# State-space layer of a two-layer backbone: two groups on the partition halves, real and imaginary parts along the free axis

## The chip, the cores and the metric

The kernel is one program on one core of a Trainium2 chip. The metric is the device time of one execution in microseconds (us), lower is better. The core has a matrix engine (TensorE; PE in the profile, PEld for its weight loads), a vector engine (VectorE, DVE), a scalar engine (ScalarE, ACT), GpSimd (POOL) and a sync engine (SP) that issues most of the DMAs here. Each engine works through its own instructions in program order and waits on semaphores for the others. Data lies in SBUF, 128 partitions wide. Products of the matrix engine land in PSUM, 128 partitions of 4096 fp32 columns, in eight banks of 512 columns.

## What is computed

A latent stream of 1024 tokens and a context of 256 tokens, model width 1024, run through two layers: a differential attention with an MLP, and a bidirectional S5 state-space mixer with a gated output (GLU) and an MLP. The change touches the S5 mixer only. Cut to it, the reference is

```python
S5_GROUP, S5_GROUPS, S5_STATE = 16, 64, 64          # 16 channels x 64 groups, 64 complex states a group
lam_bar = exp(lam * dt);  b_bar = ((lam_bar - 1) / lam)[..., None] * (b_re + 1j * b_im)
def step(h, uc):                                     # over chunks of time, forwards and backwards
    bu = einsum('gpc,btgc->btgp', b_bar, uc)
    hs = scan(a=lam_bar, b=bu) + a_cum * h           # h[t] = lam_bar * h[t-1] + bu[t]
    y = real(einsum('gcp,btgp->btgc', c_mat, hs))
y_lat = glu(y_forward + y_backward + d_skip * h_lat) # gelu, one matrix product, o1 * sigmoid(o2)
```

Context tokens are run ahead of the latent ones in each direction; the output is the latent stream.

## The kernel before

The program first does the attention layer, and beside it, on engines that are free, it makes tables for the S5 mixer and writes them to DRAM: `s5_prep` (decay and angle of each state), `s5_tables` (a record per set of four groups, `recd`: input weights X, output weights W), `s5_phases` (integer phases, `ptd`). The last part of layer 0 is its second MLP product, in whose time most of these tables are made. Then comes `s5()`, then `glu()` and the MLP of layer 1.

`s5()` turns time into eight parts of 128 steps, which are laid along the columns of a tile `U`, and treats the 64 groups in 16 sets of four. One turn `n` of its loop (L1811 and on) does a set; turns overlap, so turn `n` holds pieces of sets `n-2` to `n+1`. The steps are written out by hand inside `self.manual()`, so their order in the code is the order on each engine. Direction `d` is 0 (forwards) or 1 (backwards). In a turn:

- `inputs(n, d)` (PE, L1755): products of the input weights with the columns of U, 160 columns a group, into the two 1024-column areas `xbank` of PSUM. One area gets the real and imaginary part, the other the same with the halves swapped. Both directions use both areas in turn.
- `phase` (POOL, L1738) makes integer phases of 128x640, `trig` (ACT, L1742 to L1744) makes sine and cosine of them, in three steps.
- `rotate(n, d)` (DVE, L1764 and L1766) multiplies the two areas by cosine and sine; POOL adds the two (L1848, L1856).
- `decay(n, d)` (ACT, L1771) writes the decay of each state into the 640 PSUM columns `r` (2048 to 2687), and `scan(n, d)` (DVE, L1775) reads them there and runs the recurrence. I write S0 and S1 for the scans of direction 0 and 1 of a turn.
- `back` (DVE L1787, POOL L1785) turns the states back by the phases.
- `outputs(n-1)` (PE): for each of four groups one product with the lag table (L1793) and four with the states of the set before (L1796), into bank 6 or 7 of PSUM by the parity of the turn.
- gelu of set `n-2` out of that bank: square (ACT L1833), L1843 on DVE, tanh and a copy (ACT L1844, L1850), the product L1864 on DVE.
- `tr` (PE, L1800): four transposes of gelu's result into the same bank, from where `tr_out` copies a high part (ACT L1804) and a low part (DVE L1805) to SBUF, in the next turn.
- In turns 8, 10, 12, 13, 14, 15, 16 and 17, `ada_half_products` (L270 to L281): 32 products of 32 columns for the modulation vectors of layer 1, a copy (ACT L273), a transpose (L274) and up to three small DVE steps.

Beside it, `load_x` and `load_w` bring the next record from DRAM (SP). PE's order at the end of a turn is `outputs(n-1)`, `inputs(n+1, 0)`, the modulation products, `tr`; `inputs(n, 1)` comes early in the next turn.

Waits between engines are set by a scheduling layer from the accesses that the program makes. Which waits it sets is seen in the lists of instructions in the section on the change.

Of the kernel before, what the change touches and what calls it, by code (L numbers as in the profile page):

```python
# [13 lines left out]
KB = 256  # L14
# [56 lines left out]
class Prog:  # L71
# [83 lines left out]
    def setup(self):  # L155
# [15 lines left out]
        self.r8 = c.tile([128, 128], F32, name="r8")  # L171
# [814 lines left out]
    def s5_prep(self):  # L986
# [60 lines left out]
        ts(dup[:, 1, 1], zi, -1.0, None, ALU.mult)  # L1047
        b = self.misc.next()
        pc = fv(5.5, 128)
        for j in range(2):  # L1050
            nc.tensor.transpose(b[:, 128 * j : 128 * j + 128], dup[:, j].rearrange("p a b -> p (a b)"), self.ident)
        v.tensor_copy(self.r8, b[:, 0:128])
        ts(pc, b[:, 128:256], PHASE, None, ALU.mult)
# [96 lines left out]
    def s5_tables(self, o, w, acc, acc2):  # L1150
# [21 lines left out]
        def matrices(i):  # L1172
            (tp, tc_, tb_), W, XT, q = ins[i % 3], Wr[i % 2], XTr[i % 2], todo[i]
            tt(W, bcast(tc_[:, :, 0:16], 2, 9), bcast(tp[:, :, 0:9], 3, 16), ALU.mult)
            tt(t4, bcast(tc_[:, :, 16:32], 2, 9), bcast(tp[:, :, 9:18], 3, 16), ALU.mult)
            tt(W, W, t4, ALU.add)
            d = q // 16
            w0 = 1 - d
            self.dma(shaped(self.recd[q % 16][:, 1536 + 512 * d : 2048 + 512 * d], (4, 128)),
                     W[:, :, w0 : w0 + 8].rearrange("p x i c -> p x (i c)"))  # L1180
# [55 lines left out]
    def s5_phases(self, o):  # L1236

        nc = self.nc
        g = nc.gpsimd.tensor_tensor
        B, P, P16 = (self.fv(x, *d).bitcast(I32) for x, d in ((o, (128, 16)), (o + 8, (128,)), (o + 8.5, (128,))))  # L1240
        self.dma(self.fv(o + 9, 128), self.phd)
        nc.vector.tensor_copy(P, self.fv(o + 9, 128))
# [452 lines left out]
    def s5(self):  # L1695
# [10 lines left out]
        rx = shaped(r, (4, 160))  # L1706
        At, Bt = self.fv(42.5, 128, 10).bitcast(I32), self.fv(47.5, 128, 16).bitcast(I32)
        A0, B0 = self.hv(46, 2, 4, 10).bitcast(I32), self.hv(47, 2, 4, 16).bitcast(I32)
        phs = [(self.fv(x, 4, 160), self.fv(x + 2.5, 4, 160)) for x in (0, 7.5, 24.5)]
        ts = [[(self.fv(x, 4, 160), self.fv((12.5, 20)[d], 4, 160)) for x in ((5, 29.5), (15, 17.5))[d]] for d in range(2)]  # L1710
        cs = [[(self.fv(x, 4, 128), self.fv(y, 4, 128)) for x, y in (((5, 32), (29.5, 34)), ((15, 22.5), (17.5, 22.5)))[d]]
              for d in range(2)]
        slots = []
        for b in (self.hv(64, 4096).bitcast(F32), self.wv(0, 4096)):
            slots.append((shaped(b[:, 0:1536], (2, 4, 192)), shaped(b[:, 1536:2560], (2, 4, 128)),
                          shaped(b[:, 2560:3072], (4, 128)), shaped(b[:, 3072:4096], (2, 4, 128)), b))
        gT = self.gT = self.hgroups()[0:2]
        x_first = self.hv(40, 1536).bitcast(F32)
# [5 lines left out]
        def load_x(n):  # L1724
            self.dma(slots[n % 2][4][:, 0:1536] if n else x_first, self.recd[n, :, 0:1536])

        def load_w(n):
            b = slots[n % 2][4]
            self.dma(b[:, 1536:2560], self.recd[n, :, 1536:2560])
            self.dma(b[:, 2560:3072], self.lagd[:, 512 * n : 512 * n + 512])  # L1730
            for h in range(2):
                self.dma(b[64 * h : 64 * h + 64, 3072:4096], self.recd[n, 64 - 64 * h : 128 - 64 * h, 1536:2560])

        def phase(n, d):

            x0, P = 64 * d + 4 * n, phs[(2 * n + d) % 3][0].bitcast(I32)
            a, b = (At[:, x0 : x0 + 4], Bt[:, x0 : x0 + 4]) if n else (A0[:, d], B0[:, d])
            pool.tensor_tensor(P.rearrange("p x (a b) -> p x a b", b=16), bcast(a, 3, 16), bcast(b, 2, 10), ALU.add)  # L1738

        def trig(n, d):  # L1740
            Ps, Pc = phs[(2 * n + d) % 3]
            act.activation(Pc, Ps.bitcast(I32), AF.Sin, scale=0.5 * UNPHASE)  # L1742
            act.activation(Ps, Ps.bitcast(I32), AF.Sin, scale=-UNPHASE)
            act.activation(Pc, Pc, AF.Square, scale=float(np.sqrt(2.0)))  # L1744

        xbank = [self.PS[:, 1024 * j : 1024 * j + 1024] for j in range(2)]

        def inputs(n, d):
            X = slots[n % 2][0] if n else shaped(x_first, (2, 4, 192))
            cols = slice(0, 160) if d == 0 else slice(32, 192)  # L1750
            for j in range(2):
                b = xbank[j]
                for i in range(4):
                    o = 176 * i
                    mm(b[:, o : o + 160], X[:, d, i, 64 * j : 64 * j + 128], U[:, 4 * n + i, cols], start=True, stop=True)  # L1755

        def rotate(n, d):
            (Ps, Pc), (t1, t2) = phs[(2 * n + d) % 3], ts[d][n % 2]
            for j, (t, P) in enumerate(((t1, Pc), (t2, Ps))):
                b = xbank[j]  # L1760
                x = bass.AP(b.tensor, b.offset + (159 if d else 0),
                            [list(b.ap[0]), [176, 4], [-1 if d else 1, 160]])
                if j:
                    v.tensor_tensor(t, x, P, ALU.mult)  # L1764
                else:
                    v.scalar_tensor_tensor(t, P, -1.0, x, ALU.add, ALU.mult)  # L1766

        def decay(n, d):

            x0 = 64 * d + 4 * n  # L1770
            act.activation(rx[:, :, 1:160], bcast(r8[:, x0 : x0 + 4], 2, 159), AF.Copy)  # L1771

        def scan(n, d):
            t1, t2 = (t.rearrange("p x n -> p (x n)") for t in ts[d][n % 2])
            v.tensor_tensor_scan(t2, r, t1, 0.0, ALU.mult, ALU.add)  # L1775

        def back(eng, n, d, j):
            Ps, Pc = phs[(2 * n + d) % 3]
            o = cs[d][n % 2][j]
            if d:  # L1780
                o = bass.AP(o.tensor, o.offset + 127, [list(o.ap[0]), [128, 4], [-1, 128]])
            h = slice(31, 159)
            t2 = ts[d][n % 2][1][:, :, h]
            if j:
                eng.tensor_tensor(o, t2, Ps[:, :, h], ALU.mult)  # L1785
            else:
                eng.scalar_tensor_tensor(o, Pc[:, :, h], -1.0, t2, ALU.add, ALU.mult)  # L1787

        def outputs(n):
            X, W1, T, W2, _ = slots[n % 2]  # L1790
            for i in range(4):
                o = self.bank(6 + n % 2)[:, 128 * i : 128 * i + 128]
                mm(o, U[:, 4 * n + i, 32:160], T[:, i], start=True, stop=False)  # L1793
# [4 lines left out]
        def tr(kb, g, b):  # L1798
            for i in range(4):
                nc.tensor.transpose(b[:, 128 * i : 128 * i + 128], ggs[kb % 2][:, 4 * g + i].rearrange("p g c -> p (g c)"), self.ident)  # L1800

        def tr_out(kb, g, b):
            hi, lo = gT[g][0][:, kb], gT[g][1][:, kb]
            act.activation(hi, b, AF.Copy, scale=0.5)  # L1804
            return lambda: v.scalar_tensor_tensor(lo, b, 0.5, hi.bitcast(F32), ALU.mult, ALU.subtract)  # L1805

        for t, c0, w in ((A0, 0, 10), (B0, 5 * KB, 16)):
            self.dma(t, self.ptd[:, c0 : c0 + 128 * w].rearrange("p (d x w) -> p d x w", d=2, w=w)[:, :, 0:4])

        load_x(0)  # L1810
        self.dma(self.fv(42.5, 13 * KB).bitcast(I32), self.ptd)  # L1811
        load_w(0)
        self.act_set("silu_and_others")
        with self.manual():
            act.activation(U[:, :, 160:192], U[:, :, 0:32], AF.Copy)
            v.memset(rx[:, :, 0:1], 0.0)
# [4 lines left out]
            inputs(0, 0)  # L1821
            load_x(1)
            load_w(1)
            for n in range(19):
                run, m = n < 16, n - 2
                gelu = 0 <= m < 16
                bank, other = self.bank(6 + n % 2), self.bank(7 - n % 2)
                y = shaped(bank, (4, 8, 16))
                lo = tr_out((n - 4) // 2, n % 2, other) if n >= 4 else None
# [15 lines left out]
                if run:  # L1845
                    inputs(n, 1)
# [27 lines left out]
                if n < 15:  # L1874
                    inputs(n + 1, 0)
                for i, (a, b) in enumerate(mods):
                    if n == b:
                        self.ada_half_products(halves[i % 2 if i > 2 else 0], 1, 2 + i // 2, i % 2, self.PS[:, 1856:1984])
                if n + 1 < 16:
                    phase(n + 1, 1)  # L1880
                if 3 <= n < 19:
                    tr((n - 3) // 2, 1 - n % 2, bank)
# [7 lines left out]
            tr_out(7, 1, bank)()  # L1890
# [402 lines left out]
```

## Time and profile before

| | |
|---|---|
| median of 3 runs | 2930.72 us (2928.89 to 2932.73) |
| the profiled execution | 2930.97 us |
| its span, first to last instruction | 2929.2 us (1.77 us less) |
| mean granted TensorE clock | 0.985 |
| PE busy | 2793.7 us (95%) |
| DVE, ACT, POOL busy | 1899.8, 1309.7, 1012.6 us |
| `s5()`, first input product to the first GLU split | 1906.87 to 2105.84 us |

A row of the timeline gives the start, the duration, engine, line, operation, the tile written and those read with their shapes, how many instructions were joined to the row, and in brackets how long the engine had been idle before it and what ended that. `PS` is PSUM, `FD` and `U` are tiles in SBUF. A row of the windows gives a stretch of time, its length, the busy time of each engine with its count of instructions, the granted clock of the TensorE (PEclk), and the share and rate of the DMA engines.

### The profile page before, as it was taken

What the parts mean: (1) busy time and instruction counts of PE and PEld (TensorE: products, weight loads), DVE (VectorE), ACT (ScalarE), POOL (GpSimd) and SP (SyncE); (2) the same over time, 40 slices, a digit from 0 to 9 for tenths busy, and PEclk for the clock granted to TensorE, in tenths of its full rate; (3) what the DMA queues carried; (4) which work ended last, traced back from release to release, by engine and by line L of the source; (5) the groups of instructions that cost most, each with busy time, mean ns of one, the idle gap of its engine ahead of it and who ended that gap; (6) DMA issues with size and microseconds to landing.
All of it is one profiled execution on the core that took longest, in us unless ns stands there. A gap on an engine that the chain in (4) does not pass through costs nothing.

```text
span 2929.2 us, 44409 instructions
## 1 busy us (share of the span) xinstructions
PE 2793.7 (95%) x16044; PEld 2320.1 (79%) x16044; DVE 1899.8 (65%) x2789; ACT 1309.7 (45%) x2412; POOL 1012.6 (35%) x911
## 2 busy tenths in 40 slices
PE   7999999999899999999999999789899999999999
PEld 5687888888777877888777788578788778887887
DVE  5466788888763654444587764788633776758566
ACT  3424556556544743333432221356434755345443
POOL 2214676676653500000100001678301333326324
PEclk9999999999899999999999999889999999999999
DMA  9855454454726455322676663569934565467544
GB/s 267 290 196 167 132 158 147 153 162 151 230 73 186 133 159 178 120 94 84 202 216 200 199 194 89 159 194 279 301 108 145 176 219 195 151 208 253 163 136 140
DMA packets 429321, 512.95 MB, mean 175 GB/s; under 512 B 57399, under 2 KB 304429, under 8 KB 427949
## 3 DMA queue, kind: packets, MB, share of 16 engines
q1 hardware_dynamic: 428716, 508.02, 55.9%
q10 hardware_dynamic: 384, 2.10, 0.3%
q8 instruction: 126, 2.06, 0.3%
q14 instruction: 95, 0.77, 0.1%
HBM read 351.29 MB, written 154.50 MB: 173 GB/s over the span
## 4 chain that ended last, share of the span: by engine, by line
PE 69%; DVE 10%; DMA 6%; issue 6%; ACT 5%; POOL 3%; SPq 1%; DVEq 0%; ACTq 0%; POOLq 0%
PE PS L132 20%; PE PS L134 20%; PE PS L133 19%; ACT F L571 2%; PE PS L536 2%; DVE F L561 2%; PE PS L1755 1%; PE PS L594 1%; DVE R L138 1%; PE PS L208 1%; PE PS L1796 1%; DVE FD L1775 1%; DMA K<-in_mlp_w 1%; DMA od<-FC 1%; SPq L80 1%
## 5 line engine op out<-in xcount | busy, mean ns | idle before, releaser
L132 PE MATMUL PS<-H,R 128*128 128x512 f32 (+1 forms) x816 | 301.6, 372 | 7.8 <-DVE FC L487 5.5
L132 PE MATMUL PS<-H 128*128 128x512 f32 x768 | 300.5, 393 | 3.3 <-ACT H L137 3.3
L134 PE MATMUL PS<-H 128*128 128x512 f32 x768 | 299.3, 391 | 2.0 <-DVE H L138 2.0
L133 PE MATMUL PS<-H 128*128 128x512 f32 x768 | 300.2, 391 | 0.0
L133 PE MATMUL PS<-H,R 128*128 128x512 f32 (+1 forms) x816 | 293.3, 360 | 1.4 <-POOL H L138 1.4
L134 PE MATMUL PS<-H,R 128*128 128x512 f32 (+1 forms) x816 | 293.1, 360 | 0.0
L132 PE MATMUL PS<-R,H 128*128 128x512 f32 x540 | 216.9, 403 | 1.7 <-ACT R L137 1.6
L571 ACT ACTIVATE F<-F,stat 128x1280 f32<-128x1280 f32 x128 | 174.3, 1362 | 98.8 <-DVE F L561 98.5
L137 ACT ACTIVATE R<-W 128x512 fp32r<-128x512 f32 (+1 forms) x184 | 131.1, 718 | 192.5 <-PE PS L133 144.6
L133 PE MATMUL PS<-R,H 128*128 128x512 f32 x540 | 212.3, 394 | 0.0
L134 PE MATMUL PS<-R,H 128*128 128x512 f32 x540 | 211.3, 395 | 0.0
L138 DVE TENSOR_TENSOR H<-W,H 128x512 fp32r<-128x512 f32 (+1 forms) x145 | 136.7, 951 | 106.9 <-ACT H L137 99.5
L561 DVE TENSOR_SCALAR_CACHE_REDUCE F<-PS 128x1280 f32<-128x1280 f32 x128 | 185.1, 1482 | 13.4 <-PE PS L536 13.3
L138 DVE TENSOR_TENSOR R<-W,R 128x512 fp32r<-128x512 f32 (+1 forms) x148 | 125.3, 852 | 102.1 <-ACT R L137 76.0
L137 ACT ACTIVATE H<-W 128x512 fp32r<-128x512 f32 (+2 forms) x166 | 107.0, 653 | 182.7 <-PE PS L133 115.1
L608 POOL TENSOR_SCALAR R<-F 128x256 fp32r<-128x256 f32 (+1 forms) x128 | 136.0, 1063 | 147.7 <-ACT F L607 134.5
L132 PEld LDWEIGHTS PS<-H,R 128*128 128x128 f32 x816 | 154.2, 189 | 37.8 <-DVE FC L487 7.2
L134 PEld LDWEIGHTS PS<-H,R 128*128 128x128 f32 x816 | 154.2, 189 | 26.2 <-POOL R L138 1.4
L536 PE MATMUL PS<-R,R 64*128 64x256 f32 (+1 forms) x1440 | 158.9, 349 | 16.1 <-DVE F L561 9.8
L132 PEld LDWEIGHTS PS<-H 128*128 128x128 f32 x768 | 144.4, 188 | 36.7 <-ACT H L137 4.1
L133 PEld LDWEIGHTS PS<-H,R 128*128 128x128 f32 x816 | 154.8, 190 | 22.5 <-POOL H L138 1.6
L134 PEld LDWEIGHTS PS<-H 128*128 128x128 f32 x768 | 144.5, 188 | 33.3 <-DVE H L138 2.8
(455 smaller groups left out, 7246.0 us busy)
## 6 DMA issues: line engine op xcount, KB each, us to landing
W<-in_mlp_w SPq DMA_DIRECT2D x192, 256.0 KB
Ad<-F SPq DMA_DIRECT2D x112, 256.0 KB
W<-Ad SPq DMA_DIRECT2D x112, 256.0 KB
W<-in_ada_w SPq DMA_DIRECT2D x34, 512.0 KB
W<-in_mlp_w SPq DMA_DIRECT2D x32, 512.0 KB
H<-hidd SPq DMA_DIRECT2D x64, 256.0 KB
U<-in_ada_w SPq DMA_DIRECT2D x32, 512.0 KB
W<-in_s_w_glu SPq DMA_DIRECT2D x64, 256.0 KB
```

The lines of the kernel that those rows point to most:

```text
L80: return self.nc.sync.dma_start(out=out, in_=in_)
L132: mm(out, ah, bh, start=first, stop=False, **kw)
L133: mm(out, ah, bl, start=False, stop=False, **kw)
L134: mm(out, al, bh, start=False, stop=last, **kw)
L137: self.nc.scalar.activation(hi, src, AF.Copy)
L138: (lo_eng or self.nc.vector).tensor_tensor(lo, src, hi.bitcast(F32), ALU.subtract)
L208: self.nc.tensor.matmul(acc[32 * j : 32 * j + 32, 0:256], self.scT[:, 2 * k : 2 * k + 32], w[:, 256 * j : 256 * j + 256], start=k == 0, st ...
L536: mm(self.PS[:, o : o + k1 - k0], Q[rows, i, qs], K[j][rows, k0:k1], start=n == 0, stop=n == 2)
L561: ts(p[c], self.PS[:, 1280 * c : 1280 * c + 1280], 1.0, None, ALU.mult, ALU.min, accum_out=sm[:, c : c + 1])
L571: nc.scalar.activation(p[c], p[c], AF.Exp, bias=sm[:, c : c + 1], scale=-1.0, accum_out=sn[:, 0:1] if c else s0[:, u + 1 : u + 2])
L594: self.nc.tensor.transpose(tb[:, 128 * (kt - k0) : 128 * (kt - k0) + 128], w[:, 128 * kt : 128 * kt + 128], self.ident)
L608: nc.gpsimd.tensor_scalar(hi, t, 1.0, 0.0, ALU.mult, ALU.add)
```

## The change

The partition halves now hold two groups, `h`, and the real and imaginary parts, `c`, lie along the free axis. A tile of 128x640 is 2 parts x 2 groups x 160 instead of 4 groups x 160, so cosine and sine are made once for both parts.

- `inputs(n, d)`: eight products of 64 columns of weights each, in pairs on the two column halves, into `xbank[d]` alone. Both directions of set `n+1` are issued at the end of turn `n`; `inputs(n, 1)` is gone from the middle of the turn. The second copy of the weights goes from the record.
- `phase` and `trig` work on 128x320; `trig` has five steps instead of three (minus sine, sine, half-angle sine, its square, less one).
- `rotate` and `back` are plain products (TENSOR_TENSOR), with the cosine read twice.
- `outputs(n-1)`: four products with the lag table over all 128 rows, and 32 over 64 rows each, which alternate between the upper and the lower half.
- PSUM: the outputs of an even set are at columns 2816 to 3327, those of an odd set at 3328 to 3839, in place of banks 6 and 7; the transposes at 1792 to 2047 and 3840 to 4095; the modulation products at 2688 to 2815 in place of 1856 to 1983. `r` stays at 2048 to 2687. With 512 columns a bank, bank 5 (2560 to 3071) holds the end of `r`, the modulation products and half of the even outputs, bank 6 half of the even and half of the odd outputs, bank 7 half of the odd outputs and half of the transposes.
- The record in DRAM is 2048 columns wide instead of 2560, and 1.25 MB instead of 2 MB are loaded a turn; X is written once. Phase tables are half as large.

```diff
@@ s5_tables
-            X = shaped(self.recd[q % 16][:, 768 * d : 768 * d + 768], (4, 192))
-            self.dma(X[:, :, 0:128], Xs)
-            self.dma(X[:, :, 128:192], Xs[:, :, 0:64])
+            self.dma(shaped(self.recd[q % 16][:, 512 * d : 512 * d + 512], (4, 128)), Xs)
@@ s5
...
         def load_w(n):
-            b = slots[n % 2][4]
-            self.dma(b[:, 1536:2560], self.recd[n, :, 1536:2560])
-            self.dma(b[:, 2560:3072], self.lagd[:, 512 * n : 512 * n + 512])
+            b = slots[n % 2][3]
+            rec = self.recd[n, :, 1024:2048].rearrange("p (d h m) -> h p d m", d=2, h=2)
             for h in range(2):
-                self.dma(b[64 * h : 64 * h + 64, 3072:4096], self.recd[n, 64 - 64 * h : 128 - 64 * h, 1536:2560])
+                for c in range(2):
+                    self.dma(shaped(b[64 * h : 64 * h + 64, 1024 + 512 * c : 1536 + 512 * c], (2, 256)), rec[h, 64 * c : 64 * c + 64])
+            self.dma(b[:, 2048:2560], self.lagd[:, 512 * n : 512 * n + 512])
...
         def trig(n, d):
             Ps, Pc = phs[(2 * n + d) % 3]
-            act.activation(Pc, Ps.bitcast(I32), AF.Sin, scale=0.5 * UNPHASE)
-            act.activation(Ps, Ps.bitcast(I32), AF.Sin, scale=-UNPHASE)
+            P = Ps[:, 1].bitcast(I32)
+            act.activation(Pc, P, AF.Sin, scale=0.5 * UNPHASE)
+            act.activation(Ps[:, 0], P, AF.Sin, scale=-UNPHASE)
+            act.activation(Ps[:, 1], P, AF.Sin, scale=UNPHASE)
             act.activation(Pc, Pc, AF.Square, scale=float(np.sqrt(2.0)))
+            act.activation(Pc, Pc, AF.Copy, bias=-1.0)
...
         def inputs(n, d):
-            for j in range(2):
-                b = xbank[j]
-                for i in range(4):
-                    o = 176 * i
-                    mm(b[:, o : o + 160], X[:, d, i, 64 * j : 64 * j + 128], U[:, 4 * n + i, cols], start=True, stop=True)
+            for c in range(2):
+                for y in range(2):
+                    o = 176 * (2 * c + y)
+                    for h in range(2):
+                        i = 2 * h + y
+                        mm(xbank[d][64 * h : 64 * h + 64, o : o + 160], X[:, d, i, 64 * c : 64 * c + 64],
+                           U[:, 4 * n + i, cols], start=True, stop=True)
...
+        def ybank(n):
+            x = 2816 + 512 * (n % 2)
+            return self.PS[:, x : x + 512]
+
         def outputs(n):
-            for i in range(4):
-                o = self.bank(6 + n % 2)[:, 128 * i : 128 * i + 128]
-                mm(o, U[:, 4 * n + i, 32:160], T[:, i], start=True, stop=False)
-                for d in range(2):
-                    for j, W in enumerate((W1, W2)):
-                        mm(o, cs[d][n % 2][j][:, i], W[:, d, i], start=False, stop=d == 1 and j == 1)
+            o = [ybank(n)[:, 128 * i : 128 * i + 128] for i in range(4)]
+            for y in range(2):
+                for h in range(2):
+                    i = 2 * h + y
+                    mm(o[i], U[:, 4 * n + i, 32:160], T[:, i], start=True, stop=False)
+                for d in range(2):
+                    for j in range(2):
+                        for c in range(2):
+                            for h in range(2):
+                                rows = slice(64 * h, 64 * h + 64)
+                                mm(o[2 * h + y], cs[d][n % 2][j][rows, c, y], W[rows, c ^ j, d, y], start=False, stop=d + j + c == 3)
...
+            inputs(0, 1)
...
-                    inputs(n, 1)
...
                     inputs(n + 1, 0)
+                    inputs(n + 1, 1)
...
-                        self.ada_half_products(halves[i % 2 if i > 2 else 0], 1, 2 + i // 2, i % 2, self.PS[:, 1856:1984])
+                        self.ada_half_products(halves[i % 2 if i > 2 else 0], 1, 2 + i // 2, i % 2, self.PS[:, 2688:2816])
```

In the changed kernel the lines are: `inputs` L1761, `rotate` L1770, `decay` L1775, `scan` L1779, `back` L1788, the lag products L1800, the other output products L1806, `tr` L1813, the high and low copies L1817 and L1818, gelu's square L1846 and product L1876.

The instructions of PE from the first output product of turn 5 on (`outputs(4)`, an even set), with the waits that each carries, in the kernel before (L1793 and L1796 are output products, L1755 the input products of set 6):

```order
L1793 MATMUL PS<-H,U 128x128 [waits DMAHW0_49,DVE_49]
L1796 MATMUL PS<-H,FD 128x128 [waits DMAHW1_49,Pool_49]
L1796 MATMUL PS<-H,FD 128x128 [waits DMAHW3_49,DMAHW2_49,Pool_49]
L1796 MATMUL PS<-H,FD 128x128
L1796 MATMUL PS<-H,FD 128x128 [waits Pool_49]
L1793 MATMUL PS<-H,U 128x128
L1796 MATMUL PS<-H,FD 128x128 x4
```

and in the changed one:

```order
L1800 MATMUL PS<-H,U 128x128 [waits DMAHW7_49,Activation_49]
L1800 MATMUL PS<-H,U 128x128
L1806 MATMUL PS<-H,FD 128x128 [waits DMAHW2_49,Pool_49]
L1806 MATMUL PS<-H,FD 128x128 [waits DMAHW3_49]
L1806 MATMUL PS<-H,FD 128x128 [waits DMAHW0_49]
L1806 MATMUL PS<-H,FD 128x128 [waits DMAHW1_49]
L1806 MATMUL PS<-H,FD 128x128 [waits Pool_49]
L1806 MATMUL PS<-H,FD 128x128 x7
L1806 MATMUL PS<-H,FD 128x128 [waits Pool_49]
L1806 MATMUL PS<-H,FD 128x128 x3
L1800 MATMUL PS<-H,U 128x128 x2
L1806 MATMUL PS<-H,FD 128x128 x16
```

Before, the first product waits for a DVE instruction, which is the low copy L1805 of the same turn. Now it waits for an ACT instruction: the semaphore value is that of `decay(6, 0)` (L1775), the last ACT write into `r`, which shares bank 5 with the even outputs. In the code that step stands just ahead of `outputs(n - 1)`, and it waits itself for S1 of the turn.

The instructions of PE that follow, up to the first output product of turn 6 (an odd set), before:

```order
L1755 MATMUL PS<-U,H 128x160 [waits DMAHW4_49,DVE_49]
L1755 MATMUL PS<-U,H 128x160 x3
L1755 MATMUL PS<-U,H 128x160 [waits DVE_49]
L1755 MATMUL PS<-U,H 128x160 x3
L1800 MATMUL PS<-ident,FD 128x128 [waits DVE_49]
L1800 MATMUL PS<-ident,FD 128x128 x3
L1755 MATMUL PS<-U,H 128x160 [waits DVE_49]
L1755 MATMUL PS<-U,H 128x160 x3
L1755 MATMUL PS<-U,H 128x160 [waits DVE_49]
L1755 MATMUL PS<-U,H 128x160 x3
L1793 MATMUL PS<-W,U 128x128 [waits DMAHW5_49,DVE_49]
```

and in the changed kernel:

```order
L1761 MATMUL PS<-U,H 64x160 [waits DMAHW4_49]
L1761 MATMUL PS<-U,H 64x160 x15
L1813 MATMUL PS<-ident,FD 128x128 x4
L1800 MATMUL PS<-W,U 128x128 [waits DMAHW5_49,DVE_49]
L1800 MATMUL PS<-W,U 128x128
```

All sixteen input products of set 6 now stand between the outputs and the transposes, and no rotation is waited for there. The first output product still waits for DVE, but for a later instruction: gelu's product L1876 of turn 6, the last reader of the even outputs, whose half lies in bank 6 beside that of the odd ones.

The instructions of DVE in turn 6, from the second rotation to the last `back`, before:

```order
L1766 SCALAR_TENSOR_TENSOR FD<-FD,PS 128x640 [waits PE_49,Activation_49]
L1764 TENSOR_TENSOR FD<-PS,FD 128x640 [waits DVE_49,PE_49,Pool_49]
L1775 SCALAR_TENSOR_TENSOR FD<-PS,FD 128x640 [waits Pool_49]
L1864 TENSOR_TENSOR U<-FD,PS 128x4x8x16 [waits Activation_49]
L1787 SCALAR_TENSOR_TENSOR FD<-FD 128x512 [waits DVE_49]
L1775 SCALAR_TENSOR_TENSOR FD<-PS,FD 128x640 [waits Activation_49,Pool_49]
L1787 SCALAR_TENSOR_TENSOR FD<-FD 128x4x128 [waits DVE_49]
```

and in the changed kernel:

```order
L1770 TENSOR_TENSOR FD<-PS,FD 128x640 [waits Activation_49]
L1770 TENSOR_TENSOR FD<-PS,FD 128x640 [waits DVE_49,Pool_49]
L1779 SCALAR_TENSOR_TENSOR FD<-PS,FD 128x640 [waits Pool_49]
L1876 TENSOR_TENSOR U<-FD,PS 128x4x8x16 [waits Activation_49]
L1788 TENSOR_TENSOR FD<-FD 128x512 [waits DVE_49]
L1779 SCALAR_TENSOR_TENSOR FD<-PS,FD 128x640 [waits Pool_49]
L1788 TENSOR_TENSOR FD<-FD 128x4x128 [waits DVE_49]
```

The rotation no longer waits for PE. S1 (the second L1779) has lost its wait for ACT, because the gelu product ahead of it now waits for the same ACT instruction, `decay(6, 1)`: the even outputs that it reads share bank 5 with `r`. Before, that product waited for gelu's own ACT step L1850.

More of the change, by code (lines that the diff above doesn't have):

```diff
@@ L1705, in s5 @@
         r = self.PS[:, 2048:2688]
[L1706 to L1711, printed above, removed]
+        rx = shaped(r, (2, 2, 160))
+        At, Bt = self.fv(42.5, 64, 10).bitcast(I32), self.fv(45, 64, 16).bitcast(I32)
+        A0, B0 = self.hv(46, 2, 2, 10).bitcast(I32), self.hv(47, 2, 2, 16).bitcast(I32)
+        phs = [(self.fv(x, 2, 2, 160), self.fv(x + 2.5, 2, 160)) for x in (0, 7.5, 24.5)]
+        ts = [[(self.fv(x, 2, 2, 160), self.fv((12.5, 20)[d], 2, 2, 160)) for x in ((5, 29.5), (15, 17.5))[d]] for d in range(2)]
+        cs = [[(self.fv(x, 2, 2, 128), self.fv(y, 2, 2, 128)) for x, y in (((5, 32), (29.5, 34)), ((15, 22.5), (17.5, 22.5)))[d]]
               for d in range(2)]
@@ L1757, in rotate @@
         def rotate(n, d):
             (Ps, Pc), (t1, t2) = phs[(2 * n + d) % 3], ts[d][n % 2]
[L1759 to L1766, printed above, removed]
+            b = xbank[d]
@@ L1768, in decay @@
+            for j, t in enumerate((t1, t2)):
+                x = bass.AP(b.tensor, b.offset + (159 if d else 0) + 352 * j,
+                            [list(b.ap[0]), [-352 if j else 352, 2], [176, 2], [-1 if d else 1, 160]])
+                v.tensor_tensor(t, x, Ps if j else bcast(Pc, 1, 2), ALU.mult)
         def decay(n, d):
-            x0 = 64 * d + 4 * n
-            act.activation(rx[:, :, 1:160], bcast(r8[:, x0 : x0 + 4], 2, 159), AF.Copy)
+            x0 = 32 * d + 2 * n
+            act.activation(rx[:, :, :, 1:160], bcast(bcast(r8[:, x0 : x0 + 2], 2, 159), 1, 2), AF.Copy)
@@ L1773, in scan @@
         def scan(n, d):
-            t1, t2 = (t.rearrange("p x n -> p (x n)") for t in ts[d][n % 2])
+            t1, t2 = (t.rearrange("p c x n -> p (c x n)") for t in ts[d][n % 2])
             v.tensor_tensor_scan(t2, r, t1, 0.0, ALU.mult, ALU.add)
@@ L1780, in back @@
             if d:
[L1781 removed]
+                o = bass.AP(o.tensor, o.offset + 127, [list(o.ap[0]), [256, 2], [128, 2], [-1, 128]])
             h = slice(31, 159)
[L1783 to L1787, printed above, removed]
[L1789 to L1796 removed]
@@ L1798, in tr @@
-        def tr(kb, g, b):
-            for i in range(4):
[L1800 to L1808, printed above, removed]
+            t2 = ts[d][n % 2][1][:, :, :, h]
@@ new lines, in back @@
+            eng.tensor_tensor(o, t2, Ps[:, :, :, h] if j else bcast(Pc[:, :, h], 1, 2), ALU.mult)
+        def ybank(n):
+            x = 2816 + 512 * (n % 2)
+            return self.PS[:, x : x + 512]
+        def outputs(n):
+            X, W, T, _ = slots[n % 2]
+            o = [ybank(n)[:, 128 * i : 128 * i + 128] for i in range(4)]
[6 more added lines that the diff above has]
+                        for c in range(2):
+                            for h in range(2):
+                                rows = slice(64 * h, 64 * h + 64)
+                                mm(o[2 * h + y], cs[d][n % 2][j][rows, c, y], W[rows, c ^ j, d, y], start=False, stop=d + j + c == 3)
@@ new lines, in s5, with tr, tr_out @@
+        trb = bass.AP(self.PS.tensor, self.PS.offset + 1792, [list(self.PS.ap[0]), [2048, 2], [1, 256]])
+        def tr(kb, g):
+            for i in range(4):
+                x = (1792, 1920, 3840, 3968)[i]
+                nc.tensor.transpose(self.PS[:, x : x + 128], ggs[kb % 2][:, 4 * g + i].rearrange("p g c -> p (g c)"), self.ident)
+        def tr_out(kb, g):
+            hi, lo = (shaped(gT[g][j][:, kb], (2, 256)) for j in range(2))
+            act.activation(hi, trb, AF.Copy, scale=0.5)
+            return lambda: v.scalar_tensor_tensor(lo, trb, 0.5, hi.bitcast(F32), ALU.mult, ALU.subtract)
@@ L1810, in s5 @@
+        for t, c0, w in ((A0, 0, 10), (B0, 640, 16)):
+            self.dma(t, self.ptd[:, c0 : c0 + 64 * w].rearrange("p (d x w) -> p d x w", d=2, w=w)[:, :, 0:2])
         load_x(0)
-        self.dma(self.fv(42.5, 13 * KB).bitcast(I32), self.ptd)
+        self.dma(self.fv(42.5, 1664).bitcast(I32), self.ptd)
         load_w(0)
@@ L1826, in s5 @@
                 gelu = 0 <= m < 16
-                bank, other = self.bank(6 + n % 2), self.bank(7 - n % 2)
-                y = shaped(bank, (4, 8, 16))
-                lo = tr_out((n - 4) // 2, n % 2, other) if n >= 4 else None
+                y = shaped(ybank(n), (4, 8, 16))
+                lo = tr_out((n - 4) // 2, n % 2) if n >= 4 else None
                 if 1 <= n <= 16:
```

49 lines of the change are left out of this document (25 added, 24 removed).

## The prediction

> **What bounds the kernel now.** I read the shares of the engines first, then the windows around the S5 loop, then the loop's timeline.
>
> ```profile
> PE 69%; DVE 10%; DMA 6%; issue 6%; ACT 5%; POOL 3%; SPq 1%; DVEq 0%; ACTq 0%; POOLq 0%
> 1408.00:1880.00 472.00, 471.20 (x2300) 378.22 (x2301) 329.99 (x426) 134.76 (x233) 50.95 (x55) 1.00 0.62 179
> 1996.00:2042.00 46.00, 42.49 (x434) 40.67 (x434) 39.24 (x49) 30.36 (x51) 35.33 (x25) 1.00 0.97 302
> ```
>
> The first row is the chain that ended last: PE carries most of it. The second is the MLP product ahead of S5, where the records and phase tables are made: PE is busy 471 of 472 us, so the table writes there lie under PE. Fewer of them can gain at most the 0.8 us that PE idles, and I take nothing. The third is a piece of the S5 loop: no engine is full there (PE 42.5, DVE 39.2 of 46), and the DMA share of 0.97 looks like a bound. But in the list of waits over the loop no engine of a turn waits for a record, so the smaller records are worth nothing by themselves (nor do five DMAs instead of four cost anything, as SP only loads ahead); the longest sum there is ACT's wait for the scans:
>
> ```profile
> ACT PS L1771 <- DVE FD L1775: 42.8, 18, 3.1
> ```
>
> What the loop costs must be read from one turn:
>
> ```profile
> 1994.68 0.69 DVE L1787 SCALAR_TENSOR_TENSOR FD<-FD 128x512 f32<-128x512 f32 x1
> 1995.56 0.60 ACT L1804 ACTIVATE H<-PS 128x512 fp32r<-128x512 f32 x1 [0.18 <-PE PS L1800]
> 1996.53 0.74 ACT L1742 ACTIVATE FD<-FD 128x640 f32<-128x640 int32 x1
> 1998.69 0.82 DVE L1766 SCALAR_TENSOR_TENSOR FD<-FD,PS 128x640 f32<-128x640 f32 x1 [0.67 <-ACT FD L1744]
> 2001.56 0.66 DVE L1864 TENSOR_TENSOR FD<-FD,PS 128x512 f32<-128x512 f32 x1
> 2001.77 0.68 ACT L1771 ACTIVATE PS<-r 128x636 f32<-128x636 f32 x1
> 2002.14 1.52 DVE L1787 SCALAR_TENSOR_TENSOR FD<-FD 128x512 f32<-128x512 f32 x1
> 2003.59 1.48 DVE L1775 TENSOR_TENSOR_SCAN FD<-PS,FD 128x640 f32<-128x640 f32 x1
> 2005.10 0.70 ACT L1771 ACTIVATE PS<-r 128x636 f32<-128x636 f32 x1 [2.64 <-DVE FD L1775]
> 2008.32 0.60 ACT L1804 ACTIVATE H<-PS 128x512 fp32r<-128x512 f32 x1 [0.85 <-PE PS L1800]
> 2016.36 1.48 DVE L1775 TENSOR_TENSOR_SCAN FD<-PS,FD 128x640 f32<-128x640 f32 x1
> ```
>
> A turn ends with S1, at 2005.10 here. From the high copy L1804 (1995.56) to that end are **9.54 us**: square, sine and cosine on ACT, second rotation (1998.69), S0, gelu's product, a `back`, S1. With decay (0.70) it makes 10.24, the whole of an ordinary turn. The next turn has modulation products, and its S1 comes at 2016.36, 12.77 after 2003.59, because its high copy waited 0.85 for PE's transposes. So ordinary turns are a chain of ACT and DVE, and PE's products lie **beside** that chain. PE in the same turn:
>
> ```profile
> 1996.16 2.44 PE L1755 MATMUL PS<-U,H 128*128 128x160 f32 x16 [0.64 <-DVE FD L1766]
> 1998.43 0.38 PE L1793 MATMUL PS<-W,U 128*128 128x128 f32 x2
> 2002.90 2.34 PE L1755 MATMUL PS<-U,W 128*128 128x160 f32 x16
> 2005.17 1.95 PE L270 MATMUL PS<-U,scT 128*32 128x128 f32 x64
> 2007.68 0.60 PE L1800 MATMUL PS<-ident,U 128*128 128x128 f32 x4
> ```
>
> The outputs run from 1998.43 to 2002.90, 4.47 us, one set of inputs 2.27 (2002.90 to 2005.17), the modulation products add 2.51 ahead of the transposes, and from those to the high copy are 0.64 (2007.68 to 2008.32).
>
> **The change, part by part.** *Work that shrinks.* Two input sets become one by time if the half-width products run in pairs: 2.27 less PE a turn. Phases halve on POOL. The sines go from three steps of 640 to five of 320: three take 2.16 (1996.53 to 1998.69), and five at half the length plus a fixed part come out within a few tenths of that either way; I take nothing. Rotations and `back` keep size and count, also nothing. Had nothing else changed, all of this would lie beside the 10.24 us chain.
>
> *The wait that is added.* The order of instructions shows it. In odd turns the first output product now waits for `decay(n+1, 0)`, which itself follows S1; in even turns for gelu's product L1876, which itself waits for `decay(n, 1)`. Queued behind on PE stand all outputs, both input sets of the next turn, the modulation products and the transposes. The next turn's first rotation waits for the inputs, its high copy for the transposes, and behind that copy on ACT stand the square, the sines, hence the rest of the 9.54 us chain. PE's work goes from beside the chain **into** it.
>
> *Its price.* From the first output product to the high copy: outputs 4.47 (four full products, and 32 half ones that in pairs cost as 16), inputs 2.27, transposes 0.64, and five changes between full, half-row and half-column shapes. For these the nearest row is PE's idle time ahead of L270, the one change of shape in this loop:
>
> ```profile
> PEld PS L270 <- issue: 0.9, 5, 0.2
> ```
>
> That is 0.9 us in five, 0.18 each, 0.9 a turn; the ends are nothing and, by twice the row, 1.8. Together 8.28. [...]
>
> - Odd turn n, S1 to S1: decay 0.76 with its latency, 8.28, 9.54: **18.6**.
> - Even turn: gelu's product starts when `decay(n, 1)` ends, 0.7 later than now, and ends some 2.2 before S1 does (POOL holds up the `back` behind it anyway: 1.52 at 2002.14 against 0.69 alone at 1994.68). So -2.2 + 8.28 + 9.54: **15.6**.
>
> *The clock.* PE then idles over 7 us in every turn. The trace has one such pause in the loop:
>
> ```profile
> 1923.62 4.63 PE L1755 MATMUL PS<-U,W 128*128 128x160 f32 x16 [7.75 <-DVE FD L1766]
> 1928.05 0.43 PE L1793 MATMUL PS<-H,U 128*128 128x128 f32 x2
> 1918.00:1922.00 4.00, 0.00 (x0) 0.00 (x0) 1.38 (x1) 2.49 (x4) 2.27 (x2) 0.50 0.00 0
> 1922.00:1926.00 4.00, 2.38 (x9) 2.38 (x10) 2.27 (x4) 3.36 (x5) 3.73 (x3) 0.50 0.02 4
> ```
>
> After 7.75 us of idling the granted clock is 0.50, and one set of input products takes 4.43 us (1923.62 to 1928.05) instead of 2.27. I add 2.2 a turn; the other end is nothing, for a PE that stays warm. [...]
>
> So odd turns take 20.8, even ones 17.8, with modulation products (2.5) 23.3 and 20.3. From S1 of turn 0 to S1 of turn 15:
>
> ```profile
> 1906.87 6.74 PE L1755 MATMUL PS<-U,H 128*128 128x160 f32 x32 [22.94 <-issue]
> 1913.64 0.82 DVE L1764 TENSOR_TENSOR FD<-PS,FD 128x640 f32<-128x640 f32 x1 [0.36 <-PE PS L1755]
> 1916.04 1.72 POOL L1738 TENSOR_TENSOR FD<-FD 128x640 int32<-128x640 int32 x1
> 1920.62 1.49 DVE L1775 TENSOR_TENSOR_SCAN FD<-PS,FD 128x640 f32<-128x640 f32 x1 [3.98 <-ACT PS L1771]
> 2088.08 1.48 DVE L1775 TENSOR_TENSOR_SCAN FD<-PS,FD 128x640 f32<-128x640 f32 x1
> 2090.97 0.60 ACT L1804 ACTIVATE H<-PS 128x512 fp32r<-128x512 f32 x1 [0.86 <-PE PS L1800]
> 2092.35 0.49 PE L1793 MATMUL PS<-W,U 128*128 128x128 f32 x2 [1.41 <-DVE H L1805]
> 2094.25 0.69 DVE L1864 TENSOR_TENSOR FD<-FD,PS 128x512 f32<-128x512 f32 x1 [1.36 <-ACT FD L1850]
> ```
>
> Now 167.5 us. After: turn 0 has no outputs (some 8.2, by DVE and ACT), turns 1 and 2 have no transposes (18.6 and 15.0, as above with the clock and without the high copy); then five odd turns of 20.8, two even of 17.8, four even of 20.3 and turn 13 of 23.3. Sum 286, **118.5 more**. *Start*: the inputs of direction 1 no longer wait for a rotation, so both sets are there 4.5 us after 1906.87, and the second rotation ends some 1.6 ahead of now (its last step starts at 1913.64); the phases behind it on POOL, which hold up the first S1, take half of 1.72. Together 2.5 less. *Tail*: the outputs of set 14 wait for the end of S1 (2089.57), so the high copy comes 4.47 + 0.9 + 2.2 + 2.5 + 0.64 = 10.7 after it instead of 1.4: 9.3 more. Those of set 15 wait for gelu's product (to 2094.94, 4.0 behind the high copy) instead of the low copy (1.4): 2.6, with shapes and clock 5.7 more. Tail 15.
>
> On the profiled execution, 2930.97 (0.25 over the median): 2930.97 + 118.5 - 2.5 + 15 = **3062 us**.
>
> **The rivals.** [...]
>
> *The pairs do not overlap.* The half-row products then cost one by one: 36 of 0.22 are 8.0, not 4.47, and the inputs 4.54, not 2.27. That is 5.8 in each of 14 turns and 7 in the tail: **3151**. Two places in the trace speak against it. L270 has 64 instructions of 32 columns in 1.95, 0.03 each, where a full one takes 0.11, so four run at once. The attention's half-row products:
>
> ```profile
> 640.28 0.28 PE L133 MATMUL PS<-R 128*128 128x256 f32 x1
> 640.40 0.28 PE L134 MATMUL PS<-R,R 128*128 128x256 f32 x1
> 645.87 2.39 PE L536 MATMUL PS<-R,R 64*128 64x256 f32 x21
> 648.19 0.66 PE L594 MATMUL PS<-ident,F 128*128 128x128 f32 x4
> L536 PE MATMUL PS<-R,R x21: 274/381/493, 645.9 to 648.0; 64*128 64x256 f32 x12, 64*128 64x512 f32 x9
> ```
>
> 256 full columns take 0.12 (640.28 to 640.40). [...]
>
> *The change does what it says, and it is faster.* The place is the first output product: if it is released as early as now, because the wait is satisfied from an earlier decay, PE stays beside the chain and has 2.3 us less to do. Ordinary turns keep their 10.24. The five with modulation products, 12.7 now, fall to PE's own 4.47 + 2.27 + 0.9 + 2.5 + 0.64, some 10.8, 9.5 together; with the start and the tail 13 less, **2918**. It decides if the first product starts before S1 in odd turns. Against it: in even turns S1 has lost its own ACT wait, which fits only if gelu's product ahead waited for the decay.
>
> **How the numbers follow.** Forecast 0.60, warm PE 0.14, unpaired products 0.13, faster 0.09, the rest, with waits that bind in some turns only, 0.04. The range of 3010 to 3150 takes in the warm PE with free changes of shape (3027 - 14) and nearly the unpaired products, and leaves out the faster case and the upper part of the unpaired one. A measurement of this kernel tells about 0.2% from no change: faster by more than that 0.09, within it 0.02, slower 0.89.
>
> **What would show it.** Right: in odd turns the first L1800 has idle time ended by ACT L1775, in even ones by DVE L1876; S1 to S1 alternates near 21 and 18; PEclk in the loop falls well below 0.90 while DVE and ACT keep their busy time and gain idle time; the high copy L1817 waits some 8 to 10 us for L1813. Outputs take 4.5 us warm if paired, 8 if not. Wrong: S1 every 10.3 us, with L1800 in the middle of the turn. Should the MLP product ahead of S5 grow or shrink by microseconds, my zero for the tables is wrong.

## The result, and the profile after

The changed kernel takes 3067.07 us (median of 5 runs, 3064.98 to 3069.73), the one before 2931.92 us (5 runs, 2928.89 to 2935.7). The ratio is **1.0461**, 95% interval 1.0446 to 1.0476: 135 us slower, where 131 were forecast (3062). The profiled execution took 3065.86 us, its span is 3064.1, 134.9 more than before.

The S5 loop as one window, from its first input product to the GLU, first of the kernel before (columns as above: length, busy PE, PEld, DVE, ACT, POOL, granted clock, DMA share, rate):

```profile
1906.80:2106.00 199.20, 174.99 (x1737) 167.23 (x1737) 159.98 (x194) 118.29 (x194) 139.98 (x94) 0.96 0.83 259
```

and of the changed one:

```profile
1906.80:2242.00 335.20, 185.03 (x2248) 164.27 (x2248) 156.04 (x195) 119.44 (x254) 117.73 (x94) 0.74 0.37 118
```

The whole loss lies here: 136 us more in the window. DVE and ACT are as busy as before, PE only 10 us more, at a lower clock (0.74 instead of 0.96). So idling was added on every engine at once, from 126 us on PE to 158 us on POOL, which is what serial work looks like. What PE, ACT and DVE waited for, in sum over the loop (line that waited, what ended the wait, us, times, longest):

```profile
PE PS L1800 <- ACT PS L1775: 74.4, 7, 14.3
ACT H L1817 <- PE PS L1813: 75.3, 15, 11.3
DVE FD L1770 <- PE PS L1761: 71.5, 10, 9.6
PE PS L1800 <- DVE U L1876: 29.5, 4, 7.9
PE PS L1800 <- DVE FD L1876: 28.3, 4, 7.9
PE PS L1800 <- DVE FD L1779: 9.6, 1, 9.6
```

The first output product L1800 waits seven times for decay, eight times for gelu's product and once (set 14) for the last S1: 142 us in sixteen turns. In return ACT waits for PE's transposes and DVE for its input products. Two turns on PE, and the steps on ACT and DVE on which they hang:

```profile
2019.85 1.22 PE L1800 MATMUL PS<-W,U 128*128 128x128 f32 x4 [7.89 <-DVE U L1876]
2021.00 3.02 PE L1806 MATMUL PS<-W,FD 64*128 64x128 f32 x32
2024.59 2.06 PE L1806 MATMUL PS<-W,FD 64*128 64x128 f32 x32
2026.57 2.39 PE L1761 MATMUL PS<-U,W 128*64 128x160 f32 x32
2029.65 0.60 ACT L1817 ACTIVATE H<-PS 128x512 fp32r<-128x512 f32 x1 [7.06 <-PE PS L1813]
2037.72 1.48 DVE L1779 TENSOR_TENSOR_SCAN FD<-PS,FD 128x640 f32<-128x640 f32 x1
2039.99 1.22 PE L1800 MATMUL PS<-H,U 128*128 128x128 f32 x4 [10.43 <-ACT PS L1775]
2041.14 3.18 PE L1806 MATMUL PS<-H,FD 64*128 64x128 f32 x32
2044.89 2.06 PE L1806 MATMUL PS<-H,FD 64*128 64x128 f32 x32
2049.20 0.66 PE L1813 MATMUL PS<-ident,U 128*128 128x128 f32 x4
2049.95 0.60 ACT L1817 ACTIVATE H<-PS 128x512 fp32r<-128x512 f32 x1 [10.02 <-PE PS L1813]
2057.74 1.22 PE L1800 MATMUL PS<-W,U 128*128 128x128 f32 x4 [7.89 <-DVE FD L1876]
2058.21 1.48 DVE L1779 TENSOR_TENSOR_SCAN FD<-PS,FD 128x640 f32<-128x640 f32 x1
```

Here the chain of the forecast can be followed by hand. Turn 7, an odd one, ends with S1 (2037.72 to 2039.20); decay follows, and at 2039.99 PE starts, after 10.43 us of idling. 9.96 us later (2049.95) comes the high copy, and from there S1 of the next turn follows as before. The outputs of that even turn start at 2057.74, when gelu's product has ended, shortly ahead of its S1. In these rows each product shows as two instructions, so a row of 32 half-row instructions is 16 products. The two such blocks of a turn hold equal work, yet the first takes 3.18 us and the second 2.06, since the clock rises between them, from 0.56 to 1.00:

```profile
2037.00:2040.00 3.00, 0.01 (x1) 0.02 (x1) 2.89 (x3) 0.70 (x1) 1.30 (x2) 0.50 0.00 0
2040.00:2044.00 4.00, 4.00 (x34) 3.77 (x36) 0.00 (x0) 0.00 (x0) 0.00 (x0) 0.56 0.02 4
2044.00:2048.00 4.00, 4.00 (x58) 3.64 (x58) 0.00 (x0) 0.00 (x0) 0.94 (x1) 1.00 0.51 136
```

The MLP product ahead of S5 is unchanged: the loop starts at 1907.13 instead of 1906.87.

### The profile page after: what moved, and what is told of

Same layout as the page of the kernel before. It is cut to its first block, busy times and chain, and to the rows that moved or that the text cites. A ratio compares the mean times of both kernels' runs of the same rounds, so it can differ in the third digit from the quotient of the medians.

```text
span 3064.1 us, 45472 instructions
## 1 busy us (share of the span) xinstructions
PE 2798.8 (91%) x16556; PEld 2312.7 (75%) x16556; DVE 1890.6 (62%) x2791; ACT 1312.6 (43%) x2476; POOL 981.5 (32%) x911
## 4 chain that ended last, share of the span: by engine, by line
PE 70%; DVE 9%; ACT 7%; DMA 6%; issue 5%; POOL 2%; SPq 0%; DVEq 0%; ACTq 0%; POOLq 0%
PE PS L132 20%; PE PS L134 19%; PE PS L133 19%; PE PS L1806 3%; ACT F L571 2%; DVE F L561 2%; PE PS L536 2%; PE PS L594 1%; PE PS L1800 1%; DVE R L138 1%; PE PS L1761 1%; PE PS L208 1%; DMA W<-in_mlp_w 1%; DMA od<-FC 1%; DVE FD L1779 1%
```

## The experiments

Two theories stood against each other. **Banks**: the outputs' new columns share PSUM banks with `r` and with the other parity, so the program waits by bank, and PE's work comes in series with ACT and DVE. **Products**: the half-width products, the changes of shape or the new order of the inputs cost the time by themselves. The first four runs shared a kernel before of 2929.88 us (7 runs).

**The old loop with shifted columns.** Only the columns of the kernel before are moved:

```diff
+        def ybank(n):
+            x = 2816 + 512 * (n % 2)
+            return self.PS[:, x : x + 512]
...
-                o = self.bank(6 + n % 2)[:, 128 * i : 128 * i + 128]
+                o = ybank(n)[:, 128 * i : 128 * i + 128]
...
-                bank, other = self.bank(6 + n % 2), self.bank(7 - n % 2)
+                bank, other = ybank(n), ybank(n + 1)
...
-                        self.ada_half_products(..., self.PS[:, 1856:1984])
+                        self.ada_half_products(..., self.PS[:, 2688:2816])
```

> The kernel before with one edit: the outputs, the transposes that share their columns and the modulation products stand at the columns of the changed kernel (2816, 3328 and 2688); full-width products, one engine order, records and phases as before. Theory (shared PSUM banks put PE's products in series with ACT and DVE): the first output product waits for decay in odd turns and for gelu's product in even ones, S1 to S1 some 19.9 and 16.9 us with the slow clock (no changes of shape, one input set in the chain), 2.5 more with modulation products: about 3050 us, 3030 to 3070. Rival (the half-width products and the new order of the inputs cost the time, the banks do not matter): within 5 us of the kernel before, 2931.

Measured 3058.13 us, ratio 1.0437 (1.0419 to 1.0454). Its waits over the loop (L1797 is the first output product there, L1771 decay, L1868 gelu's product):

```profile
PE PS L1797 <- ACT PS L1771: 51.3, 7, 8.2
PE PS L1797 <- DVE FD L1868: 21.1, 4, 5.5
PE PS L1797 <- DVE U L1868: 19.7, 4, 5.5
```

Without one half-width product, with the old order and the old records, other columns alone cost 128 us (3058.13 less 2929.88), nearly all that the change costs. The same two waits appear, seven and eight times. From turn 3 on, S1 to S1 takes 19.1 to 20.5 us in odd turns without modulation products and 16.7 and 17.1 in even ones (19.9 and 16.9 expected). The rival (2931) is out.

**Decay in banks of its own.** The changed kernel, with inputs and `r` moved:

```diff
-        r = self.PS[:, 2048:2688]
+        r = self.PS[:, 1408:2048]
...
-        xbank = [self.PS[:, 1024 * j : 1024 * j + 1024] for j in range(2)]
+        xbank = [(self.PS[:, 0:688], 176), (self.PS[:, 704:1344], 160)]
```

(the transposes go to 2048 and 3840, the modulation products to 2304).

> The changed kernel with the input areas packed into columns 0 to 1343 and the decay columns r moved to 1408 to 2047, so that r shares no bank with the outputs; even and odd outputs still share bank 6. Theory: the wait for decay goes, that for gelu's product of the same turn stays, in odd and even turns alike: S1 to S1 some 14.9 us warm, 17.1 with the slow clock, 2.5 more with modulation products: about 3023 us, 3005 to 3040. Rival (sharing with r is not what binds): as the changed kernel, 3067. Rival (r was all of it): under 2960.

Measured 3033.57 us (1.0352, 1.0337 to 1.0368), 10 over the forecast and within its range. The wait for decay is gone from L1800, and gelu's product has taken over all fifteen turns that have one:

```profile
PE PS L1800 <- DVE U L1876: 43.1, 8, 6.8
PE PS L1800 <- DVE FD L1876: 37.6, 7, 6.8
```

S1 to S1 is 17.0 to 17.6 us in odd and even turns alike (17.1 forecast), no longer 21 and 18. So decay was about a quarter of the loss, as far as the shared output banks let it show.

**No shared output banks.** In addition even outputs in banks 4 and 5, odd ones in 6 and 7:

```diff
-            x = 2816 + 512 * (n % 2)
-            return self.PS[:, x : x + 512]
+            x = 2048 + 1024 * (n % 2)
+            return self.PS[:, x : x + 1024].rearrange("p (i k) -> p i k", i=4)[:, :, 0:128]
```

(the transposes go to the other halves of banks 4 and 5, the modulation products to 3200, in bank 6).

> As the run before, and the even outputs in banks 4 and 5, the odd ones in banks 6 and 7, 128 of every 256 columns, so that no output bank is shared with r or with the other parity. Part of the second input set still shares a bank with r, so those products wait for decay, with the transposes behind them. Theory: the outputs run beside ACT and DVE again, PE stays warm, S1 to S1 some 11.7 us, 14.2 with modulation products: about 2943 us, 2930 to 2960. Rival (half-width products or the slow clock cost the time by themselves): over 3000.

Measured 2958.28 us (1.0094, 1.0078 to 1.0109): 109 us of the 135 are back, with every half-width product in place, so the second theory (over 3000) is out. Ordinary turns take 11.7 to 12.4 us. What is left shows on PE: it stands before the part of the second input set that shares bank 2 with `r`, and the transposes stand behind it.

```profile
1979.75 1.85 PE L1761 MATMUL PS<-U,W 128*64 128x160 f32 x24
1985.15 0.76 PE L1761 MATMUL PS<-U,W 128*64 128x160 f32 x8 [3.55 <-ACT PS L1775]
1985.85 0.66 PE L1813 MATMUL PS<-ident,FD 128*128 128x128 f32 x4
```

**Transposes first.** In addition:

```diff
                     inputs(n + 1, 0)
+                if 3 <= n < 19:
+                    tr((n - 3) // 2, 1 - n % 2)
+                if n < 15:
                     inputs(n + 1, 1)
...
-                if 3 <= n < 19:
-                    tr((n - 3) // 2, 1 - n % 2)
```

> As the run before, with the transposes issued ahead of the second input set in each turn. Theory: ordinary turns fall to some 10.4 us, the chain of ACT and DVE alone; turns with modulation products stay near 13.3, since their ACT copy stands ahead of the high copy: about 2929 us, 2918 to 2940, 10 to 15 us under the run before. Rival (the transposes behind the inputs do not bind there): the same time as the run before.

Measured 2944.46 us (1.0049, 1.0034 to 1.0064), 14 under the run before, as forecast, though both runs are 15 us over their numbers, this one over its range too. Ordinary turns are mostly at 10.2 (two at 11.1, one at 12.8), those with modulation products at 13.5 to 14.7, and from the last S1 to the GLU it takes 26.7 us, before 17.8.

**Modulation products apart, two tries.** The ACT copy of these products stood ahead of the high copy. First it was moved behind the sines of the next turn, and PE's transpose of it behind that turn's outputs.

> As the run with the transposes first, and of the modulation products the ACT copy stands behind the sines of the next turn, and PE's transpose with the DVE steps behind that turn's outputs, so that no high copy waits for them. Theory: turns with modulation products (13.5 us there) fall to 10.3 to 11, the loop from 174 us to some 157, and the tail by some 4: about 2922 us, 2914 to 2930, under the kernel before. Rival (PE is full in those turns and the products cost 2.5 wherever they stand): 2940 to 2945.

Measured 2936.07 us (12 runs) against 2931.5: 1.0018 (1.0009 to 1.0026). A miss of 14 us: the turns stayed at up to 14.8, for two waits not foreseen, since the products' columns lay in bank 6 with the odd outputs (L1868 and L1855 are gelu's sum and square there, L278 the copy, L270 the products):

```profile
DVE FD L1868 <- ACT adat L278: 18.1, 5, 5.0
ACT FD L1855 <- PE PS L270: 13.4, 5, 3.7
```

The second try puts these columns into bank 4, the transposes into 6 and 7, and the products between the two parts of the second input set.

> As the run with the late copy, where that copy and the products' columns held up gelu of the odd outputs through bank 6. Now the modulation products have columns in bank 4 and the transposes in banks 6 and 7, the products stand between the two parts of the second input set, the ACT copy behind gelu's square, PE's transpose behind the others of its turn. Theory (shared banks again): turns with modulation products 10.3 to 11.2 instead of 10.2 to 14.8, the loop some 160 instead of 173: about 2923 us, 2916 to 2930. Rival (PE is full in those turns): 2936 as that run.

Measured 2931.92 us (11 runs) against 2932.23: **0.9997** (0.9988 to 1.0007), no difference from the kernel before, and a miss of 9 us. Ordinary turns take 10.2 (two of them 10.8), those with modulation products 11.2 to 14.7. In its profile the loop takes 165.2 us from the first S1 to the last (167.5 before), but from there to the GLU 22.0 (17.8 before). The profile shows two things that the expectation left out. The products of one modulation vector wait five times, 6.1 us in all, for the DVE step that reads those of the one before out of the same columns. And PE is slow in places, with a granted clock of 0.91 in the mean from 1906.8 to 2080: here, after 2.46 us of waiting, 32 half-row instructions take 3.79 us, where 32 of them took 2.06 a turn earlier (from 2035.36). In the changed kernel such a row takes 3.79 at a granted clock of 0.50 (from 2058.89).

```profile
2043.70 0.76 PE L1769 MATMUL PS<-U,H 128*64 128x160 f32 x8 [1.04 <-ACT PS L1783]
2046.93 1.23 PE L1808 MATMUL PS<-W,U 128*128 128x128 f32 x4 [2.46 <-DVE H L1826]
2048.08 3.79 PE L1814 MATMUL PS<-W,FD 64*128 64x128 f32 x32
```

**PE kept busy.** The changed kernel, with products that nobody uses in PE's pauses:

```diff
                     rotate(n, 0)
+                    if 3 <= n < 15:
+                        for _ in range(24):
+                            mm(self.PS[:, 704:832], self.ident, self.ident, start=True, stop=True)
```

> The changed kernel, and in turns 3 to 14 PE gets 24 added products of 128 columns (some 5.4 us, results unused) behind the first rotation, in the time in which it waits. Theory (slow clock after the pauses): the granted clock of the loop stays near 1, from the first output product to the high copy 8.3 to 8.6 us instead of some 9.9: 12 turns by 1.3 to 2.2 less, about 3045 us, 3038 to 3053. Rival (the pauses cost only the waiting): 3067, or more by what the added products delay.

Measured 3053.44 us (1.0418, 1.0402 to 1.0433), just above its range and 14 under the changed kernel, with a loop of 272.6 instead of 288.8 us from the first S1 to the last. The clock over the loop is 0.88, not near 1. Where it stays up, as in six of the twelve turns, the first output product to the products behind the inputs takes 7.58 us (2056.01 to 2063.59). Elsewhere it takes 9.0 to 9.5, and the pause need not be longer:

```profile
2018.17 1.22 PE L1800 MATMUL PS<-W,U 128*128 128x128 f32 x4 [2.28 <-DVE U L1879]
2019.32 3.00 PE L1806 MATMUL PS<-W,FD 64*128 64x128 f32 x32
2056.01 0.71 PE L1800 MATMUL PS<-W,U 128*128 128x128 f32 x4 [2.28 <-DVE FD L1879]
2056.65 2.06 PE L1806 MATMUL PS<-W,FD 64*128 64x128 f32 x32
2063.59 1.96 PE L270 MATMUL PS<-U,scT 128*32 128x128 f32 x64
```

The same with 36 products in odd turns. The pause there was still 4.8 us in turns 5 and 7 and 3.5 in turn 13; in turns 3, 9 and 11 it was 1.7 to 2.0, and PE had started at full clock (in turns 9 and 11 the high copy waited 8.38 and 8.39 for the transposes, in turn 7 9.97):

> As the run with 24 added products in each turn, and 36 in odd turns, whose pause was still 4.8 us long there. Theory (a pause of 4.8 us is long enough for the slow clock, one of 2.3 us is not): the first output products of odd turns run warm too, 1.3 to 2.2 us less in each of six turns: about 3042 us, 3038 to 3047. Rival (the remaining slow start has another cause): 3053 as that run.

Measured 3058.16 us (1.0429, 1.0412 to 1.0446). A miss: the loop took 272.9 us, as in the run before. In turns 5 and 7 the pause had shrunk to 2.1 and 2.2, and PE still started slow (9.17 us up to the transposes); turn 13, after 0.8, started at full clock (the ACT copy of the modulation products waited 9.71 there, 11.31 in the run before). In turns 3, 9 and 11 the added products now delay the first output product, which starts 1.3 to 1.7 us behind the end of S1 instead of 0.8. So the length of the last pause alone does not decide. The 5 us over that run lie ahead of the loop in its profile (first S1 at 1924.2 instead of 1919.9), where the two kernels are alike.

**Halves one after the other.** The changed kernel with the loop over `h` moved outside those over `d`, `j` and `c` in `outputs`:

> The changed kernel with the half-row output products in another order: all eight of the upper half, then all eight of the lower one, instead of one by one in turn. Theory (halves that alternate run at the same time): 16 pairs come apart, 0.11 each warm and twice that cold: 3.5 to 5 us more in each of 16 turns, about 3130 us, 3110 to 3150. Rival (they did not overlap anyway): 3067.

Measured 3222.38 us (1.0992, 1.0978 to 1.1006): 155 more, where 63 were expected: a miss. A block of 32 takes 6.4 us, not 2.0, and the granted clock stays at 0.50, although PE works without a pause (the last two rows are windows of 4 us):

```profile
2043.49 6.51 PE L1806 MATMUL PS<-H,FD 64*128 64x128 f32 x32
2049.93 1.22 PE L1800 MATMUL PS<-H,U 128*128 128x128 f32 x4
2046.00:2050.00 4.00, 4.00 (x23) 3.78 (x22) 0.00 (x0) 0.00 (x0) 0.00 (x0) 0.50 0.00 0
2054.00:2058.00 4.00, 4.00 (x25) 3.75 (x25) 0.00 (x0) 0.00 (x0) 0.33 (x1) 0.50 0.20 66
```

The slow clock alone would not do that: at the same granted clock of 0.50, an alternating block of the changed kernel takes 3.72 us (2083.15 to 2086.87, clock 0.50 from 2083 to 2087), this one 6.44. So alternating halves do run at the same time, and that rival is settled by measurement. By these rows the lost overlap is worth some 5.4 us a turn (3.5 to 5 expected), an estimate of 87 us in sixteen turns; the rest would be the clock that stays low (0.58 from 1906.8 to 2400, in the changed kernel 0.74 over the loop), which the expectation did not count on.

## Why the prediction was right, point by point

| term | forecast | measured |
|---|---|---|
| start of S5 to first S1, less | 2.5 | 2.9 (10.81 for 13.75) |
| first S1 to last S1, more | 118.5 | 121.4 (288.85 for 167.46) |
| last S1 to the GLU, more | 15 | 17.4 (35.17 for 17.76) |
| ahead of S5 and behind it | 0 | -1.0 |
| span | +131 | +134.9 |

- **The added wait** is shown, not only argued: it is in the waits of the changed kernel, it appears in the old loop when its columns alone are moved, and it goes, with 109 us, when the columns are moved apart.
- **Its price**, PE's 8.28 us from first output product to high copy at full clock: up to the transposes the forecast has 7.64 (8.28 less 0.64), and the run with PE kept busy shows 7.58 up to the next products in each of turns 3 to 14 that starts at full clock. The row behind the changes of shape is one of the weight loads (PEld), not of the products, so it was no direct reading. Pairs, changes of shape and inputs were sized well together; what a change of shape costs by itself no run shows.
- **The clock** was put at 2.2 a turn, from one restart at which sixteen input products were slow. Up to the products behind the inputs the changed kernel takes 9.05 to 10.52 us in turns 3 to 14 (9.21 in turn 7, 2039.99 to 2049.20) and 9.73 in the mean. Less the 7.58 that is 1.5 to 2.9 a turn, and 2.15 in the mean. So the term was right in the mean; that a single restart came so near it, with turns that scatter so widely, is luck. No run shows the 3027 less 14 at the lower end of the range, for a PE that stays at full clock (2.2 less in sixteen places, 35 in all) with changes of shape that cost nothing: with PE kept busy the kernel came to 3053.44 us, at a granted clock of 0.88 over the loop.
- **The turns**, each counted from its S1 to the next: odd ones without modulation products took 20.5 to 21.8 us (20.8 forecast), even ones 17.4 and 18.0 (17.8), even ones with modulation products 20.1 to 21.5 (20.3), turn 13 took 23.5 (23.3). Each kind lies within 0.4 of its forecast in the mean. Single turns are off by up to 1.2, mostly where the clock rose late or early (in turn 8 it was still 0.50 from 2062.6 to 2063.7, in turn 7 it was 1.00 from 2044 on): turns 3 and 8, the furthest above, are also the two with the longest way to the products behind the inputs, 10.52 and 10.43. A small part is a wait that the forecast left out: behind odd turns, S1's end followed the high copy after 9.74 us instead of 9.54, as gelu's product waited for decay.
- **The tail** was short by 2.4 us. Its first two steps came as forecast within 0.6, but the third was left at nothing:

```profile
2208.32 1.22 PE L1800 MATMUL PS<-H,U 128*128 128x128 f32 x4 [9.63 <-DVE FD L1779]
2219.54 0.60 ACT L1817 ACTIVATE H<-PS 128x512 fp32r<-128x512 f32 x1 [0.95 <-PE PS L1813]
2234.21 0.60 ACT L1817 ACTIVATE H<-PS 128x512 fp32r<-128x512 f32 x1 [0.85 <-PE PS L1813]
2236.07 1.96 PE L270 MATMUL PS<-U,scT 128*32 128x128 f32 x64 [1.90 <-DVE H L1818]
2241.96 1.99 ACT L137 ACTIVATE R<-W 128x1024 fp32r<-128x1024 f32 x2
```

From the last but two high copy (2234.21) to the GLU are 7.75 us, before 5.67 (2100.17 to 2105.84): the last modulation products now wait 1.90 for a low copy.

- **The faster rival**, 2918 if the waits did not bind: with the output waits removed and the modulation products rearranged the kernel came to 2931.9 us, no gain. Ordinary turns were held at 10.2 us by ACT and DVE, as the forecast said. The gain that it saw in turns with modulation products did not come, in two tries; whether a third order would bring it was not tried.

## What to carry to other kernels

When buffers in PSUM are moved, list for each bank who writes and reads it in a turn: two buffers that share no column can still put their engines in series, through the waits that the program gets (128 us here). Work that lay beside the longest chain was worth nothing here when halved (PE's inputs, with the waits gone: 2931.92 us against 2932.23), and cost its full length when a wait put it into the chain (9.73 us a turn in the mean, from the first output product to the products behind the inputs). A cheap test is to give the old kernel the new columns alone.

## What the runs showed of the hardware that was not expected

- Half-row instructions that alternate between the halves took 0.062 us each at full clock (32 in 1.98, 2024.59 to 2026.57) and 0.12 at a granted clock of 0.50 (32 in 3.72, 2083.15 to 2086.87); one half after the other, 0.20 each at 0.50 (32 in 6.44). In that last run the granted clock stayed at 0.50 through over 14 us in which PE was busy all the time (2043.49 to 2058). The clock does not follow PE's busy time in the profile alone.
- After the same pause of 2.28 us PE started slow in one turn (3.00 us for 32 half-row instructions) and at full clock in another (2.06). What decides it stays open.
